# Projections with the weight as the stationary operand, log decays by a triangular matrix on TensorE, and a planner that chooses among 28 plans

## The chip, the cores and the metric

One core of a Trainium2 chip runs the whole step as one program. The metric is the device time in microseconds (us) of one execution; a run is quoted with the median of several.

## The reference, cut to what matters

Four layers, each a token mixer and then a SwiGLU feed-forward block, over two streams of 128 tokens of width 1024: context (s = 0) and latents (s = 1). All weights are float32.

```python
def swiglu(h, w_in, w_out):                      # D_FF = 2816, four layers
    gate, up = jnp.split(h @ w_in, 2, -1)
    return (jax.nn.silu(gate) * up) @ w_out

# layer 0, gated DeltaNet
q, k, v, z = jnp.split(h @ w_in, 4, -1)
qkv = jax.nn.silu(dwconv_centred(jnp.concatenate([q, k, v], -1), conv_w))   # 3 taps along the tokens

# layer 3, RWKV-7
r, k, v = jnp.einsum('sbtd,sde->sbte', xm[:3], w_rkv)
w = -jax.nn.softplus(-(w0[:, None, None, :] + lora(xm[3], w1, w2, jnp.tanh))) - 0.5
decay = jnp.exp(-jnp.exp(w.astype(F32)))         # per token, channel and direction
a = jax.nn.sigmoid(a0[:, None, None, :] + lora(xm[4], a1, a2, lambda x: x))
```

Layers 1 and 2 are a neighbourhood attention and a latent attention. Layers 0 and 3 are linear recurrences in both directions, computed per head as one block of 128 tokens: products between the tokens, the inverse of a unit triangular matrix, and products with it.

## The kernel before

**Two steps.** The model's code does not issue instructions. `Tape` records them, `Plan` (line 1652) orders them, `emit` (line 2009) issues them in that order, so every instruction has the line of `emit`, 2032 (2103 in the changed kernel). `Plan` is a list scheduler: each operation has a cost and a rank (the length of the work behind it), each engine takes the ready operation of highest rank, and tiles come from rooms with fixed numbers of slots (`ROOM`, line 501: 25 of `b`, 128x1024 float32, three of `ada`, 128x2048, seven PSUM banks `acc`). `best(rounds, waits)` (line 1970) plans forwards, takes new ranks from a walk backwards, and repeats; with `ROUNDS = 9` and one value of `WAIT`, 1800, it makes nine plans, and `trunk_kernel` emits the shortest by the planner's own count. Every engine then runs its list in order.

**Weights.** A weight tile comes in by a transfer on SyncE's queue, and `split` (line 261) makes two tiles of it in the fast float32r type: `hi`, a rounded copy by ScalarE (ACT), and `lo`, the rest, by VectorE (DVE). Each product is then three multiplies on TensorE (PE): x_hi with hi, x_hi with lo, x_lo with hi. Multiplies in plain float32, as in RWKV, run as two passes each; a transpose is one pass.

**`linear` (line 296), token-major.** For each 512 columns of the weight and each stream the activations, 128x128, are stationary and the weight's 512 columns move. The result has tokens on the partitions. Stream 1 follows stream 0 by a lag of some weight tiles (`FIN`, `IN`), which hold their slots until then.

**FFN, `ffn_` (line 453).** `w_in` is taken in 11 chunks of 512, gate and up in turn, the last chunk 256 of each. Gate goes through Silu on ACT, up is multiplied on DVE, and `to_T` (line 360) transposes the 128x512 result on PE (four transposes) and splits it for `linear_k` with `w_out`.

**DeltaNet, `deltanet_` (line 637).** `w_in` has eight chunks: q, k, v two each, then z. `evac` (line 733) copies a chunk, transposes it to channel-major, does the three taps there (one ACT and two DVE instructions for each of four blocks), applies Silu and transposes back. `unit` normalises and transposes q and k; the score products follow (PE, 128x256 plain float32), then the inverse (`inverses`, line 583): two STREAM_TRANSPOSEs on DVE, a serial chain of 62 small DVE instructions (`substitute`), two more transposes, then 256 PE passes of 32x32 (`inverse_64`).

**RWKV, `rwkv_` (line 1188).** Channel halves g = 0, 1 and directions d = 0, 1. `rw_decays` (line 1402) makes, channel-major, the log decay and a: for each of w and a, four 64-row multiplies and four Tanh; for w then a sum along the tokens by scans on DVE, the subtraction of the middle token's value, and exponentials. `rw_keys`, `rw_products` and `inverse` follow, once for g = 0 and once for g = 1; `core(g, d)` uses the results.

**Filler.** `ada_group` (line 217) makes the modulation vectors of this and the next layer: 32 multiplies for a group, four to each 1 MB tile of `ada_w`. `fill` records two or three groups in each mixer, and the planner sets them where it likes.

Of the kernel before, what the change touches and what calls it, by code (L numbers as in the profile page):

```python
# [18 lines left out]
FF = 2816  # L19
# [77 lines left out]
class Trunk:  # L97
# [224 lines left out]

    def linear_k(self, W, xs, evac, lags=None, done=None, whole=False):
# [129 lines left out]
    def ffn_(self, l):  # L453
# [5 lines left out]
        chunks = []  # L459
        for c in range(5):  # L460
            chunks += [[(c * 512, c * 512 + 512)], [(FF + c * 512, FF + c * 512 + 512)]]
        chunks += [[(2560, FF), (FF + 2560, 2 * FF)]]
        sil = {}

        def evac(ci, s, ps):
            if ci < 10 and ci % 2 == 0:
                sil[s] = self.g([128, 512])
                nc.scalar.activation(sil[s], ps, AF.Silu)
                return
            c = ci // 2  # L470
            if c == len(hid):
                hid.append([self.g([128, 4, 2, 128], F32R) for _ in range(2)])
            with self.scope():
                m = self.g([128, 512])
                if ci < 10:
                    nc.vector.tensor_tensor(m, ps, sil[s], op=OP.mult)
                    self.free(sil[s])
                    n = 4
                else:
                    t = self.g([128, 512])  # L480
                    nc.scalar.activation(t[:, :256], ps[:, :256], AF.Silu)
                    nc.vector.tensor_tensor(m[:, :256], ps[:, 256:], t[:, :256], op=OP.mult)
                    n = 2
                self.to_T(m, n, hid[c][0][:, :n, s, :], hid[c][1][:, :n, s, :])
        self.linear(W, chunks, xs, evac, FIN)
# [23 lines left out]
ROUNDS = 9  # L509
WAIT = 1800.0  # L510
# [5 lines left out]
class DeltaNet:  # L516
# [120 lines left out]
    def deltanet_(self, l):  # L637
# [95 lines left out]
        def evac(ci, s, ps):  # L733
            which, half = ci // 2, ci % 2
            if which == 3:
                nc.scalar.activation(zs[s][half].rearrange("p a b -> p (a b)"), ps, AF.Silu)
                return
            with self.scope():
                tok = self.g([128, 512])
                nc.scalar.activation(tok, ps, AF.Copy)  # L740
                p = self.ps()
                for i in range(4):
                    nc.tensor.transpose(p[:, i * 128:(i + 1) * 128], tok[:, i * 128:(i + 1) * 128], self.ident)
                x = p.rearrange("p (a b) -> p a b", b=128)
                cv = self.g([128, 4, 128])
                for i in range(4):
                    c = ci * 4 + i
                    nc.scalar.activation(cv[:, i], x[:, i], AF.Copy, scale=cw[:, 1, c:c + 1])
                    nc.vector.scalar_tensor_tensor(cv[:, i, 1:], x[:, i, :127], cw[:, 0, c:c + 1], cv[:, i, 1:], op0=OP.mult, op1=OP.add)
                    nc.vector.scalar_tensor_tensor(cv[:, i, :127], x[:, i, 1:], cw[:, 2, c:c + 1], cv[:, i, :127], op0=OP.mult, op1=OP.add)  # L750
                nc.scalar.activation(cv, cv, AF.Silu)
                p = self.ps()
                for i in range(4):
                    nc.tensor.transpose(p[:, i * 128:(i + 1) * 128], cv[:, i], self.ident)
                h0 = half * 4
                dst = (qk[s][which][:, h0:h0 + 4] if which < 2 else V[s][half]).rearrange("p a b -> p (a b)")
                nc.scalar.activation(dst, p, AF.Copy)
                if which < 2:
                    sq = self.g([128, 512])
                    nc.scalar.activation(sq, p, AF.Square)  # L760
                    nc.vector.tensor_reduce(ss[:, s, which, h0:h0 + 4], sq.rearrange("p (a b) -> p a b", b=128), axis=AX.X, op=OP.add)
            if ci == 3:
                unit(s)
            if ci == 5 and s == 1:
                decays()
# [33 lines left out]
        self.linear(I["dn_w_in"][j], [[(c * 512, c * 512 + 512)] for c in range(8)], xs, evac, IN)  # L799
# [380 lines left out]
class Rwkv:  # L1180
# [7 lines left out]
    def rwkv_(self, l):  # L1188
# [4 lines left out]
        r = self.g([96, 128])  # L1193
        for at, n, v in ((0, 48, I["rw_mu"][j].rearrange("i (k p) -> (i k) p", p=128)),
                         (48, 8, I["rw_k_a"][j].rearrange("(k p) -> k p", p=128)),
                         (56, 8, I["rw_r_k"][j].rearrange("(k e) d -> k (e d)", e=2)),
                         (64, 16, I["rw_w0"][j].rearrange("z (k p) -> (z k) p", p=128)),
                         (80, 16, I["rw_a0"][j].rearrange("z (k p) -> (z k) p", p=128))):
            nc.gpsimd.dma_start(r[at:at + n], v)
        p = self.ps()  # L1200
        nc.tensor.transpose(p[:, :96], r, self.ident[:96, :96])
        self.free(r)
        cols = self.g([128, 96])
        nc.vector.tensor_copy(cols, p[:, :96])
# [6 lines left out]
        self.rw_b0 = {"w": cols[:, 64:80].rearrange("p (z k) -> p z k", z=2), "a": cols[:, 80:96].rearrange("p (z k) -> p z k", z=2)}  # L1211
# [35 lines left out]
        wa = self.g([128, 2, 2, 128])  # L1247

        def lora(i, nm):
# [14 lines left out]
            t = hid[nm] = wa[:, "wa".index(nm)] if nm != "g" else self.g([128, 2, 128])  # L1264
# [78 lines left out]
        lora(4, "a")  # L1343
        k = project(1, mk, KLAGS)
# [25 lines left out]
        r = project(0, mr, RLAGS)  # L1370
# [6 lines left out]
        rT = features(r)  # L1377
# [24 lines left out]
    def rw_decays(self, g, d, hid, w2):  # L1402
# [5 lines left out]
        act = {}  # L1408
        for nm in "wa":
            o = self.g([128, 4, 2, 128])  # L1410
            for h in range(2):
                p = self.ps()
                for i in range(2):
                    nc.tensor.matmul(p[:, i * 256:i * 256 + 256], w2[nm][rows, (2 * h + i) * 128:(2 * h + i + 1) * 128],
                                     hid[nm][rows].rearrange("p s t -> p (s t)"), start=True, stop=True, tile_position=(64 * d, 0))
                for i in range(2):
                    c = g * 4 + 2 * h + i
                    nc.scalar.activation(o[:, 2 * h + i].rearrange("p s t -> p (s t)"), p[:, i * 256:i * 256 + 256], AF.Tanh,
                                         bias=self.rw_b0[nm][:, d, c:c + 1], scale=0.5)
            act[nm] = o  # L1420
        sg, al = act["w"], act["a"]
        seq = lambda t: t.rearrange("p c s t -> p (c s) t")

        cm = self.g([128, 4, 2, 128])
        fl = lambda t: t.rearrange("p c s t -> p (c s t)")
        nc.vector.tensor_scalar(fl(sg), fl(sg), 1.0, None, op0=OP.add)
        a, b = (fl(sg), fl(cm)) if d == 0 else (fl(sg)[:, ::-1], fl(cm)[:, ::-1])
        shp = [128, 8, 128]
        for h in (0, 512):
# [631 lines left out]
```

## Time and profile before

| | us |
|---|---|
| median of 3 runs | 1683.51 (1679.96 to 1689.08) |
| the profiled execution | 1688.48 |
| its span | 1686.7 |
| PE busy | 1587.1 (94%) |
| DVE busy | 1128.2 (67%) |
| ACT busy | 830.3 (49%) |

The times below are of the profiled execution, from the start of its span. A PE row's length runs from the start of its first multiply to the modelled end of the last, and multiplies overlap: a long run divided by its count gives their spacing, while the mean time of one is longer. Of the layers, the DeltaNet mixer takes about 0 to 277 us, RWKV about 1160 to 1490; FFN blocks lie at about 277, 630, 963 and 1491.

### The profile page before, as it was taken

How to read it: one execution, taken by the hardware profiler on the slowest of the kernel's cores; microseconds unless marked ns; L12 is line 12 of the kernel's file. 1: busy time of each engine (PE TensorE's matmuls, PEld its weight loads, DVE VectorE, ACT ScalarE, POOL GpSimd, SP SyncE). 2: the span in 40 equal slices, each digit the busy share in tenths (PEclk: the TensorE clock that was granted, in tenths of full speed). 3: DMA queues.
4: the chain of work that ended last, by engine and by line, in shares of the span. 5: the costliest groups of instructions: out<-in, count | busy, mean ns of one | idle time of the engine just before them, and what ended most of it. 6: DMA issues, size and time to landing. Idle time of an engine off the chain costs nothing.

```text
span 1686.7 us, 24968 instructions
## 1 busy us (share of the span) xinstructions
PE 1587.1 (94%) x9396; PEld 1206.5 (72%) x9396; DVE 1128.2 (67%) x2364; ACT 830.3 (49%) x1466; POOL 63.3 (4%) x109
## 2 busy tenths in 40 slices
PE   6999689999999899999998999999999499999998
PEld 2877267888767658887775688886657378878886
DVE  4788868545486675445798854548797878675554
ACT  4798166434455664444565644433545432354443
POOL 2001010000002000000000000001010010000000
PEclk9999899999999999999999999999998779999999
DMA  9665888545658684455767854557120452335553
GB/s 364 226 215 195 325 307 319 200 147 183 208 215 269 195 299 158 169 175 204 249 215 255 334 165 174 187 200 253 59 101 10 166 195 82 114 119 178 164 193 130
DMA packets 130601, 333.79 MB, mean 198 GB/s; under 512 B 18321, under 2 KB 32466, under 8 KB 119216
## 3 DMA queue, kind: packets, MB, share of 16 engines
q1 hardware_dynamic: 123888, 311.33, 52.4%
q0 software_dynamic: 6592, 20.86, 4.2%
q8 instruction: 74, 1.21, 0.3%
q14 instruction: 47, 0.39, 0.1%
HBM read 328.25 MB, written 3.90 MB: 197 GB/s over the span
## 4 chain that ended last, share of the span: by engine, by line
PE 73%; DVE 12%; DMA 8%; ACT 5%; issue 2%; SPq 0%; ACTq 0%; DVEq 0%
PE v L2032 73%; DVE v L2032 12%; DMA v<-ada_w 5%; ACT v L2032 4%; DMA v<-ffn_w_out 2%; DMA v<-na_w_qkv 1%; DMA v<-dn_w_in 1%; ACT L2032 0%; DMA v<-ffn_w_in 0%; SPq L2032 0%; ACTq L2057 0%; ACTq L2032 0%; DVEq L2032 0%
## 5 line engine op out<-in xcount | busy, mean ns | idle before, releaser
L2032 PE MATMUL v<-v,v 128*128 128x512 f32 (+13 forms) x9364 | 1582.6, 369 | 94.1 <-DVE v L2032 44.5
L2032 PEld LDWEIGHTS v<-v,v 128*128 128x128 f32 (+6 forms) x9364 | 1200.4, 170 | 473.2 <-issue 148.7
L2032 DVE TENSOR_TENSOR v<-v,v 128x512 f32<-128x512 f32 (+19 forms) x1271 | 864.4, 705 | 477.5 <-ACT v L2032 280.8
L2032 ACT ACTIVATE v<-v 128x512 f32<-128x512 f32 (+9 forms) x989 | 679.1, 721 | 797.2 <-PE v L2032 373.6
L2032 ACT ACTIVATE v<-v,v 128x128 f32<-128x128 f32 (+2 forms) x212 | 77.3, 413 | 30.4 <-PE v L2032 12.5
L2032 DVE SCALAR_TENSOR_TENSOR v<-v,v,v 128x127 f32<-128x127 f32 (+4 forms) x200 | 66.9, 381 | 7.1 <-ACT v L2032 6.1
L2032 ACT ACTIVATE v<-v,v,v 128x128 f32<-128x128 f32 (+2 forms) x136 | 55.4, 476 | 23.6 <-DVE v L2032 23.3
L2032 DVE TENSOR_REDUCE v<-v 128x4 f32<-128x512 f32 (+4 forms) x76 | 47.1, 626 | 18.0 <-PE v L2032 12.9
L2032 POOL DMA_DIRECT2D v<-v x22 | 11.8, 535 | 780.5 <-PE v L2032 633.9
L2032 DVE TENSOR_SCALAR v<-v 128x1 int32<-128x1 int32 (+9 forms) x194 | 32.8, 175 | 9.1 <-ACT v L2032 6.1
L2032 DVE SCALAR_TENSOR_TENSOR v<-v,v 128x1 f32<-128x1 f32 (+7 forms) x156 | 32.6, 218 | 4.8 <-ACT v L2032 2.2
L2032 ACT ACT_TABLE_LOAD x22 | 28.2, 1283 | 2.4 <-DVE v L2032 1.4
L2032 POOL MEMSET v<- 128x512 f32 (+3 forms) x26 | 15.6, 618 | 330.4 <-PE v L2032 182.4
L2032 DVE SCALAR_TENSOR_TENSOR v<-v 128x1 f32<-128x1 f32 (+4 forms) x171 | 26.2, 159 | 2.5
L2032 DVE TENSOR_SCALAR v<-v,v,v 128x128 f32<-128x128 f32 x64 | 25.0, 404 | 2.0 <-PE v L2032 1.5
L2032 DVE STREAM_TRANSPOSE v<-v 128x1024 f32<-128x1024 f32 x12 | 23.4, 2003 | 3.8 <-ACT v L2032 3.6
L2032 DVE TENSOR_SCALAR v<-v,v 128x512 f32<-128x512 f32 (+2 forms) x68 | 24.6, 395 | 0.4
L2032 DVE TENSOR_TENSOR v<-v 128x1 f32<-128x1 f32 (+4 forms) x74 | 11.7, 160 | 10.9 <-ACT v L2032 9.7
L2032 DVE COPY v<-v 128x32 f32<-128x32 f32 (+9 forms) x34 | 7.5, 223 | 12.8 <-PE v L2032 12.6
L2032 ACT ACTIVATION_READ_ACCUMULATOR v<-v,v 128x1 f32 x64 | 13.3, 208 | 0.0
L2032 DVE TENSOR_TENSOR_SCAN v<-v,v 128x512 f32<-128x512 f32 x8 | 9.2, 1206 | 0.1
L2032 PE MATMUL v<-v 128*128 128x256 f32 x32 | 8.0, 378 | 0.0
(39 smaller groups left out, 62.5 us busy)
## 6 DMA issues: line engine op xcount, KB each, us to landing
v<-ada_w SPq DMA_DIRECT2D x88, 1024.0 KB
v<-ffn_w_in SPq DMA_DIRECT2D x160, 512.0 KB
v<-ffn_w_out SPq DMA_DIRECT2D x88, 512.0 KB
v<-dn_w_in SPq DMA_DIRECT2D x32, 512.0 KB
v<-na_w_qkv SPq DMA_DIRECT2D x24, 512.0 KB
v<-rw_w_rkv SPq DMA_DIRECT2D x24, 512.0 KB
v<-v POOLq DMA_DIRECT2D x20, 512.0 KB, 7.0
v<-ada_w SPq DMA_DIRECT2D x16, 512.0 KB
```

What stands on the lines that cost most here:

```text
L2032: ins = getattr(getattr(nc, engine), method)(*[real(a) for a in args], **{k: real(a) for k, a in kw.items()}).ins
```

## The change

1. `linear_T` is new: the weight's 128x128 blocks are stationary, and the activations of both streams (256 columns) move. The result is channel-major, for both streams at once, and there is no lag.
2. FFN: the first pair of chunks (`TM = 1`) stays token-major; the other ten chunks go through `linear_T`, and their result needs no transpose.
3. DeltaNet: q, k and v go through `linear_T`; the first copy and transpose go, and the taps are taken for both streams in one instruction. z stays token-major.
4. RWKV: `w0` becomes a row of the weight (a row of ones in `hid`). The log decay is made token-major by one multiply for each stream, and the sum along the tokens, relative to the middle one, by four multiplies with a triangular matrix `rw_tri`. The scans, the subtraction and some copies go; POOL sets the middle column to 1. The r projection is done channel-major, and its transposes go.
5. The planner makes 14 rounds for each of two waits, 28 plans.

```diff
+    def linear_T(self, W, chunks, ht, evac):
+        ...
+        for ci, chunk in enumerate(chunks):
+            ...
+            banks = [self.ps() for _ in range(width // 256)]
+            for k0 in range(0, nk, 2):
+                hi, lo = self.weight([W[k0 * 128:(k0 + 2) * 128, a:b] for a, b in pieces], 2, width)
+                for kk in range(2):
+                    ...
+                        nc.tensor.matmul(o, hi[:, kk, c], xh, start=(k == 0 and i % 2 == 0), stop=False)
+                        nc.tensor.matmul(o, hi[:, kk, c], xl, start=False, stop=False)
+                        nc.tensor.matmul(o, lo[:, kk, c], xh, start=False, stop=(k == nk - 1 and i % 2 == 1))
+                self.free(hi, lo)
+            evac(ci, banks)
...
-        self.linear(W, chunks, xs, evac, FIN)
+        self.linear(W, [[x] for c in range(TM) for x in pair(c)], xs, evac, FIN)
...
+        self.linear_T(W, [x for c in range(TM, 5) for x in pair(c)] + [[(2560, FF), (FF + 2560, 2 * FF)]], ht, evac)
...
-ROUNDS = 9
-WAIT = 1800.0
+TM = 1
+ROUNDS = 14
+WAITS = (900.0, 3000.0)
...
-                tok = self.g([128, 512])
-                nc.scalar.activation(tok, ps, AF.Copy)
-                p = self.ps()
-                for i in range(4):
-                    nc.tensor.transpose(p[:, i * 128:(i + 1) * 128], tok[:, i * 128:(i + 1) * 128], self.ident)
...
-                    nc.vector.scalar_tensor_tensor(cv[:, i, 1:], x[:, i, :127], cw[:, 0, c:c + 1], cv[:, i, 1:], op0=OP.mult, op1=OP.add)
+                    nc.vector.scalar_tensor_tensor(cv[:, i, :, 1:], x[:, :, :127], cw[:, 0, c:c + 1], cv[:, i, :, 1:], op0=OP.mult, op1=OP.add)
...
+        self.linear_T(W, [(c * 512, c * 512 + 512) for c in range(6)], ht, evac)
+        self.linear(W, [[(c * 512, c * 512 + 512)] for c in (6, 7)], xs, gating, IN)
...
-        for h in (0, 512):
-            nc.vector.tensor_tensor_scan(b[:, h:h + 512], self.seg, a[:, h:h + 512], 0.0, op0=OP.mult, op1=OP.add)
...
+            nc.tensor.matmul(p, hid["w"][d][:, s], w2["w"][d], start=True, stop=True)
+            with self.scope():
+                sg = self.g([128, 512])
+                nc.scalar.activation(sg, p, AF.Tanh, scale=0.5)
+                nc.vector.tensor_scalar(sg, sg, 1.0, None, op0=OP.add)
+                q = self.ps()
+                for c in range(4):
+                    nc.tensor.matmul(q[:, c * 128:c * 128 + 128], sg[:, c * 128:c * 128 + 128], self.rw_tri[:, d], start=True, stop=True)
+            q = q.rearrange("p (c t) -> p c t", c=4)
+            nc.scalar.activation(AR[s][:, :, 1], q, AF.Exp, scale=-KAPPA / 2)
+            nc.scalar.activation(cm[:, :, s], q, AF.Exp, scale=KAPPA / 2)
...
+            nc.gpsimd.memset(AR[s][:, :, 1, m:m + 1], 1.0)
+            nc.gpsimd.memset(cm[:, :, s, m:m + 1], 1.0)
...
-        r = project(0, mr, RLAGS)
+        rT = project_T(0, mr)
...
-    _, order, turns, _ = min(Plan(tape).best(ROUNDS, (WAIT,)), key=lambda x: x[0])
+    _, order, turns, _ = min(Plan(tape).best(ROUNDS, WAITS), key=lambda x: x[0])
```

The new plan moves work on every engine. Three places on PE, where `out<-moving or weight tiles` carry running numbers. In the first FFN block, the kernel before has stretches of 128x512, and two transposes (`v_75` is the identity matrix) between two chunks:

```order
L2032 MATMUL v_3382<-v_3311,v_2729 128x512
L2032 MATMUL v_3382<-v_3296,v_2815 128x512
L2032 MATMUL v_3382<-v_3296,v_2729 128x512
L2032 MATMUL v_3382<-v_3311,v_2729 128x512
L2032 MATMUL v_3382<-v_3296,v_2815 128x512
L2032 MATMUL v_3417<-v_75,v_3054 128x128 x2
L2032 MATMUL v_3422<-v_3238,v_2721 128x512
L2032 MATMUL v_3422<-v_3244,v_2721 128x512
L2032 MATMUL v_3422<-v_3238,v_2796 128x512
```

The changed kernel has the same products as 128x256, and no transpose behind the first pair of chunks:

```order
L2103 MATMUL v_3379<-v_2826,v_3307 128x256
L2103 MATMUL v_3379<-v_2875,v_3307 128x256
L2103 MATMUL v_3379<-v_2826,v_3320 128x256
L2103 MATMUL v_3366<-v_2826,v_3307 128x256
L2103 MATMUL v_3366<-v_2875,v_3307 128x256
L2103 MATMUL v_3366<-v_2826,v_3320 128x256
L2103 MATMUL v_3366<-v_2826,v_3307 128x256
L2103 MATMUL v_3366<-v_2875,v_3307 128x256
L2103 MATMUL v_3366<-v_2826,v_3320 128x256
```

In DeltaNet, just ahead of the first 32x32 of the inverse. 32x512 are the filler, 128x128 products with the initial state, `v_75` transposes. Before:

```order
L2032 MATMUL v_1671<-v_1779,v_63 32x512 x4
L2032 MATMUL v_1822<-v_1791,v_63 32x512 x4
L2032 MATMUL v_1822<-v_1804,v_63 32x512 x4
L2032 MATMUL v_1845<-v_1537,v_1212 128x128
L2032 MATMUL v_1845<-v_1562,v_1212 128x128
L2032 MATMUL v_1845<-v_1537,v_1212 128x128
L2032 MATMUL v_1845<-v_1562,v_1212 128x128
L2032 MATMUL v_1822<-v_1813,v_63 32x512 x4
L2032 MATMUL v_1822<-v_1847,v_63 32x512 x4
L2032 MATMUL v_1888<-v_75,v_1819 128x128 x4
L2032 MATMUL v_1822<-v_1861,v_63 32x512 x4
L2032 MATMUL v_1905<-v_1855,v_1479 32x32 x4
```

Changed:

```order
L2103 MATMUL v_1863<-v_1629,v_1364 128x128
L2103 MATMUL v_1870<-v_1614,v_1364 128x128
L2103 MATMUL v_1870<-v_1629,v_1364 128x128
L2103 MATMUL v_1870<-v_1614,v_1364 128x128
L2103 MATMUL v_1870<-v_1629,v_1364 128x128
L2103 MATMUL v_1900<-v_1780,v_63 32x512 x4
L2103 MATMUL v_1900<-v_1798,v_63 32x512 x4
L2103 MATMUL v_1900<-v_1815,v_63 32x512 x4
L2103 MATMUL v_1941<-v_75,v_1897 128x128 x4
L2103 MATMUL v_1900<-v_1919,v_63 32x512 x4
L2103 MATMUL v_1900<-v_1933,v_63 32x512 x4
L2103 MATMUL v_1988<-v_1957,v_1568 32x32 x6
```

Between the last score product (128x256) and the first 32x32 stood 64 filler multiplies, 20 of z (128x512), 32 with the state and four transposes; now 48 filler, 48 of z, 24 with the state and eight transposes: 28 z multiplies moved behind the scores, 16 filler multiplies moved behind the inverse.

In RWKV, ahead of the first 32x32 of the second inverse (g = 1). 128x64 and 64x64 belong to `core(0, 1)`. Before:

```order
L2032 MATMUL v_12097<-v_11065,v_11018 128x256
L2032 MATMUL v_12101<-v_11065,v_11018 128x256
L2032 MATMUL v_12097<-v_11065,v_11018 128x256
L2032 MATMUL v_12101<-v_11065,v_11018 128x256
L2032 MATMUL v_12109<-v_11065,v_11018 128x256 x2
L2032 MATMUL v_10675<-v_12056,v_63 32x512 x4
L2032 MATMUL v_10675<-v_12068,v_63 32x512 x4
L2032 MATMUL v_12195<-v_12190,v_11931 32x32 x8
L2032 MATMUL v_12195<-v_12190,v_11940 32x32 x8
```

Changed:

```order
L2103 MATMUL v_13477<-v_13516,v_12383 64x64
L2103 MATMUL v_13493<-v_12674,v_13462 128x64 x4
L2103 MATMUL v_13455<-v_13486,v_63 32x512 x4
L2103 MATMUL v_13477<-v_13542,v_12479 64x64 x8
L2103 MATMUL v_13570<-v_75,v_13452 128x128 x4
L2103 MATMUL v_13578<-v_12286,v_12241 128x256
L2103 MATMUL v_13581<-v_12286,v_12241 128x256
L2103 MATMUL v_13578<-v_12286,v_12241 128x256
L2103 MATMUL v_13581<-v_12286,v_12241 128x256
L2103 MATMUL v_13493<-v_13516,v_13490 128x64 x8
L2103 MATMUL v_13455<-v_13533,v_63 32x512 x4
L2103 MATMUL v_13607<-v_13585,v_13246 32x32 x8
```

Between the last product that feeds the inverse and its first 32x32 stood 20 filler multiplies and 45 others (122 passes in all); now 56 filler multiplies and 112 others (328 passes): most of `core(0, 1)` and 36 more filler multiplies moved here.

## Rows read from the trace of the kernel before

**Rows 1.** The page: span and PE's busy time.
```profile
span 1686.7 us, 24968 instructions
...
PE 1587.1 (94%) x9396; PEld 1206.5 (72%) x9396; DVE 1128.2 (67%) x2364; ACT 830.3 (49%) x1466; POOL 63.3 (4%) x109
```

**Rows 2.** Who PE waited for, whole run: total us, times, longest.
```profile
PE v L2032 <- DVE v L2032: 44.5, 24, 21.9
PE v L2032 <- DMA v<-ada_w: 19.4, 18, 3.3
```

**Rows 3.** Stretches: length, busy us of PE, PEld, DVE, ACT, POOL; clock, DMA share, GB/s.
```profile
277.00:427.00 150.00, 150.00 (x673) 122.58 (x674) 82.48 (x86) 65.14 (x82) 1.07 (x2) 1.00 0.55 189
...
1320.00:1357.00 37.00, 13.22 (x236) 10.63 (x236) 33.45 (x72) 11.02 (x22) 0.54 (x1) 0.64 0.42 162
```

**Rows 4.** Timeline of PE, float32r runs and transposes: start, us, what, count.
```profile
299.73 30.44 PE L2032 MATMUL v<-v,v 128*128 128x512 f32 x132
...
838.16 4.40 PE L2032 MATMUL v<-v,v 128*128 128x288 f32 x32
...
43.77 0.64 PE L2032 MATMUL v<-v,v 128*128 128x256 f32 x4
...
401.05 1.36 PE L2032 MATMUL v<-v,v 128*128 128x128 f32 x11
```

**Rows 5.** PE by form, 43.70 to 44.20 us: busy us, mean ns of one.
```profile
L2032 PE MATMUL v<-v,v 128*128 128x256 f32 x6 | 0.9, 287 | 0.0
```

**Rows 6.** Timeline of PE, runs of plain float32 passes (two to a multiply).
```profile
1216.12 15.18 PE L2032 MATMUL v<-v,v 128*128 128x512 f32 x35
...
1188.26 4.91 PE L2032 MATMUL v<-v,v 128*128 128x256 f32 x22
...
1193.75 1.78 PE L2032 MATMUL v<-v,v 64*128 64x256 f32 x14
...
1316.73 2.35 PE L2032 MATMUL v<-v,v 128*32 128x512 f32 x20
```

**Rows 7.** DVE by form, whole run: busy us, mean ns, idle before.
```profile
L2032 DVE TENSOR_TENSOR v<-v,v 128x512 f32<-128x512 f32 x326 | 214.2, 685 | 126.0 <-PE v L2032 107.8 <-ACT v L2032 10.2 <-DMA v<-na_rel_bias 5.7
...
L2032 DVE SCALAR_TENSOR_TENSOR v<-v,v,v 128x127 f32<-128x127 f32 x96 | 29.2, 344 | 6.5 <-ACT v L2032 5.7
...
L2032 DVE TENSOR_TENSOR_SCAN v<-v,v 128x512 f32<-128x512 f32 x8 | 9.2, 1206 | 0.1
...
L2032 DVE SCALAR_TENSOR_TENSOR v<-v,v,v 128x256 f32<-128x256 f32 x42 | 17.5, 478 | 0.1
```

**Rows 8.** Timeline of PE around DeltaNet's inverse; the brackets give the wait before.
```profile
156.66 0.81 PE L2032 MATMUL v<-v 128*128 128x256 f32 x3
...
203.52 1.51 PE L2032 MATMUL v<-v,v 128*32 128x512 f32 x8 [3.31 <-DMA v<-ada_w]
```

**Rows 9.** Who PE waited for from 164 to 205 us.
```profile
PE v L2032 <- DMA v<-ada_w: 9.3, 5, 3.3
PE v L2032 <- DVE v L2032: 5.7, 2, 4.9
```

**Rows 10.** Timeline of DVE: the last transposes of DeltaNet's inverse.
```profile
193.66 3.90 DVE L2032 STREAM_TRANSPOSE v<-v 128x1024 f32<-128x1024 f32 x2
```

**Rows 11.** Timeline of PE around RWKV's second inverse.
```profile
1321.89 8.40 PE L2032 MATMUL v<-v,v 128*128 128x64 f32 x76 [2.37 <-ACT v L2032]
1352.18 1.03 PE L2032 MATMUL v<-v,v 32*32 32x32 f32 x31 [21.89 <-DVE v L2032]
```

**Rows 12.** Timeline of DVE in the same stretch: the inverse itself.
```profile
1321.25 3.92 DVE L2032 STREAM_TRANSPOSE v<-v 128x1024 f32<-128x1024 f32 x2 [2.93 <-ACT v L2032]
...
1326.64 23.35 DVE L2032 TENSOR_TENSOR v<-v,v 128x31 f32<-128x31 f32 x62
1350.02 3.79 DVE L2032 STREAM_TRANSPOSE v<-v 128x1024 f32<-128x1024 f32 x2
```

**Rows 13.** Timeline of POOL in RWKV: a transfer, the wait ahead of it.
```profile
1313.35 0.55 POOL L2032 DMA_DIRECT2D v<-rw_ln_b  x1 [18.23 <-DVE v L2032]
```

More of the change, by code (lines that the diff above doesn't have):

```diff
@@ L458, in ffn_ @@
         hid = []
[L459 to L462, printed above, removed]
+        pair = lambda c: [(c * 512, c * 512 + 512), (FF + c * 512, FF + c * 512 + 512)]
         sil = {}
         def evac(ci, s, ps):
-            if ci < 10 and ci % 2 == 0:
+            if ci % 2 == 0:
                 sil[s] = self.g([128, 512])
@@ L755, in evac @@
[L755 to L761, printed above, removed]
+                for s in range(2):
+                    p = self.ps()
+                    for i in range(4):
+                        nc.tensor.transpose(p[:, i * 128:(i + 1) * 128], cv[:, i, s], self.ident)
+                    dst = (qk[s][which][:, h0:h0 + 4] if which < 2 else V[s][half]).rearrange("p a b -> p (a b)")
+                    nc.scalar.activation(dst, p, AF.Copy)
+                    if which < 2:
+                        sq = self.g([128, 512])
+                        nc.scalar.activation(sq, p, AF.Square)
+                        nc.vector.tensor_reduce(ss[:, s, which, h0:h0 + 4], sq.rearrange("p (a b) -> p a b", b=128), axis=AX.X, op=OP.add)
+                        self.free(sq)
@@ L762, in evac @@
             if ci == 3:
-                unit(s)
-            if ci == 5 and s == 1:
+                unit(0)
+                unit(1)
+            if ci == 5:
                 decays()
@@ L1246, in rwkv_ @@
         hid = {}
-        wa = self.g([128, 2, 2, 128])
+        hid["w"] = [self.g([128, 2, 128]) for _ in range(2)]
+        for d in range(2):
+            nc.gpsimd.memset(hid["w"][d], 0.0)
+            nc.gpsimd.memset(hid["w"][d][64 - 64 * d:65 - 64 * d], 1.0)
         def lora(i, nm):
@@ L1263, in lora @@
             self.free(w)
-            t = hid[nm] = wa[:, "wa".index(nm)] if nm != "g" else self.g([128, 2, 128])
+            if nm == "w":
+                for d in range(2):
+                    rows = slice(64 * d, 64 * d + 64)
+                    nc.scalar.activation(hid["w"][d][rows].rearrange("p s t -> p (s t)"), acc[rows, :256], AF.Tanh)
+                return
+            t = hid[nm] = self.g([128, 2, 128])
             f = t.rearrange("p s t -> p (s t)")
@@ L1407, in rw_decays @@
         rows = slice(64 * d, 64 * d + 64)
[L1408 to L1420, printed above, removed]
```

150 lines of the change are left out of this document (96 added, 54 removed).

## The prediction

> **What bounds the kernel now.** I read the page first [rows 1]: TensorE (PE) is busy for 1587.1 of 1686.7 us. The list of waits [rows 2] tells what holds PE in the rest: DVE for 44.5 us, of which one wait alone is 21.9, and transfers of `ada_w`, the filler's weights, for 19.4. The stretches [rows 3] show the two kinds of place. In an FFN block PE is busy for 150.00 of 150.00 us: there only PE's own instructions count, and work taken from DVE or ACT is worth nothing. From 1320 to 1357 us PE is busy for 13.22 of 37.00: there the serial inverse on DVE counts, and what the planner puts under it. So the change has two questions: does PE's own work become less, and does the new order cover the two inverses better?
>
> **PE's own work, step by step.** Transposes: 36 go in each FFN block, 48 in DeltaNet, 16 in RWKV, 208 in all. A run of eleven took 1.36 us [rows 4]. Multiplies overlap, so a run of n ends one multiply's own length, about 0.29 us [rows 5], after the last of n - 1 spacings: the transposes stand (1.36 - 0.29)/10 = 0.11 us apart. PE is busy around them, so the whole counts: 208 x 0.11 = 22.9 us less.
>
> Narrow multiplies: 2016 float32r multiplies of 512 columns (432 in each FFN block, 288 in DeltaNet) become 4032 of 256. The 512s stand (30.44 - 0.29)/131 = 0.2302 us apart. For 256 columns the trace has four in a row at full clock: (0.64 - 0.29)/3 = 0.118, on three intervals only. The 288s have more: (4.40 - 0.29)/31 = 0.1326. The line through 288 and 512 has 0.436 ns a column and meets 256 at 0.119 [rows 4, 5]. I take 0.118: two cost 0.236 for one of 0.2302, and 2016 x 0.0058 = 12 us more. The ends: half of a 512, 0.1151, would make this 0; the 288s' own spacing would make it 2016 x (0.2652 - 0.2302) = 71 us more.
>
> What could hurt is the weight load, since each multiply has its own and there are twice as many. The rows say that it hides: the same line leaves 7 ns a multiply at no columns, and a transpose, 128 columns with a load of its own, already stands 0.11 from the next [rows 4]. So the load's floor is at most 0.11, under 0.118, but only just.
>
> The Trainium skill ("TensorE: Matmul & The Clock Gate", section "The mechanism") speaks against this change: a weight load overlaps running multiplies only where the row group differs, which full-height blocks never give. The trace disagrees, with those 7 ns.
>
> RWKV's decays: in each of the four cases of g and d two plain 512s and eight plain 128s come in, 16 and 64 passes in all. At 15.18/35 = 0.43 and at 0.11 (taken from the transposes, also one pass of 128) that is 6.9 + 7.0 = 13.9 us. Sixteen half-height multiplies, 32 passes, go; those run two abreast, 1.78/14 = 0.13 each, 4.1 us. So +9.8 us. The r projection turns 64 passes of 512 into 128 of 256: 64 x 0.43 = 27.5 against 128 x 0.216 = 27.6, nothing [rows 6].
>
> The sum of PE's work: -22.9 + 12 + 9.8 = -1. By place it is -5.8 in the four FFN blocks together (144 x 0.11 less 1728 x 0.0058), -3.6 in DeltaNet and +8.0 in RWKV.
>
> **DVE and ACT.** The taps on 256 columns instead of 128 save 96 x 0.344 - 48 x 0.478 = 10 us of DVE, the scans 8 x 1.206 = 9.6 [rows 7]. I cost this at nothing by itself: PE covers it. It counts only where it starts an inverse earlier, which is in the next two terms. If PE's cover were gone in DeltaNet or RWKV, these 20 us are the most that it would be worth.
>
> **DeltaNet's inverse.** The last score product ends at 156.66 + 0.81 = 157.5; the filler group that stands last before the 32x32 ends at 203.52 + 1.51 = 205.0 [rows 8]. DVE had the inverse ready at 193.66 + 3.90 = 197.6 [rows 10], so PE was 7.5 us late, and it was so because its list stood still on `ada_w` for 9.3 us and on DVE for 5.7 [rows 9]. The new order has 12 tiles of filler there instead of 16 and 28 more z multiplies, whose weights come on the same queue but ahead. PE's work in the stretch stays near 28 us. At best the stretch shrinks by the 7.5 us, since DVE's 40 us from the scores to the inverse stay; at worst the four tiles put off cost the same waits later, four at the mean of 9.3/5 = 1.9 us, which is +7.4 with nothing gained. I take -5.
>
> **RWKV's second inverse.** From the first transpose at 1321.25 to the first 32x32 at 1352.18 is 30.9 us of DVE, and the serial chain of 62 takes 23.35 of them [rows 12]. PE had 8.40 us of work, waited 2.37 before it and 21.89 after it: 24.3 us lost [rows 11]. The new order puts 328 passes under this inverse where 122 stood. The run of 76 mixed passes took 8.40 us and the filler 2.35 us for 20 passes, some 0.11 us each [rows 6, 11], so the added 206 are worth about 20 us. Against that, eight 128x512 DVE instructions of `core` now stand inside the serial chain: at 0.685 us [rows 7], 5.5 us. So of 24.3 us lost about 10 remain, and I take -13. The ends: -20 (all 20 us fit, and the eight fit into gaps) and -3 (the added work waits for its own chain of PE, ACT and DVE, as `core` does elsewhere). What is late next is that chain, or the 14 filler tiles of this stretch. Three lie ready in their slots; at 162 GB/s for a share of 0.42 [rows 3] the queues would give some 386 GB/s at a full share (an estimate), and 11 tiles of 1.05 MB then take 30 us, less than the stretch has.
>
> The clock was 0.64 of full speed from 1320 to 1357 [rows 3], after PE had stood still; with the hole mostly filled some of that work runs at 2.4 instead of 1.2 GHz. Of 13.22 busy us I take 2 back (0 to 4).
>
> **The sum.** -1 - 5 - 13 - 2 = -21 us. The profiled execution took 1688.48 us and its span 1686.7, so 1.8 us lie around it, which the change does not touch: 1667.5 for that execution. The median of the runs is 5.0 us below it: 1662.5, say 1663. The order of everything else is new too. Of the waits in [rows 2], 17 us on DVE and 10 on `ada_w` lie outside the two inverses; I let the new plan win or lose a third, 8 us either way.
>
> **Rivals.** First, slower: the narrow multiply is bound by its weight load. At 0.118 the load's 0.11 hides by 8 ns, and any unevenness between the two shows at once. The price is 4032 times what it stands above 0.118: at the 288s' 0.1326 [rows 4] +59 us, 1722. From 0.123 on the 21 us are gone, from 0.126 it is slower than before by over 0.5%. For it: over four in ten of PE's multiplies would sit so near the floor, and the only direct reading has three intervals. Against: the 288s, with a load each, show none of it. 6%.
>
> Second, the same: the holes are filled with work that waits itself, so that the gain at both inverses is 3 us, and PE's own work gives 1: about 1680. For it: work under an inverse needs DVE, which the inverse holds. Against: the moved work in RWKV is mostly multiplies and filler. 13%.
>
> Third, POOL: it now sets the middle column of each decay, and `rw_keys` on DVE waits for that. In the new order the last four of g = 1 stand behind a transfer of `rw_ln_b`, before which POOL waited for 18.23 us [rows 13]. Were that wait to fall there, keys and the second inverse would be late by up to 18 us: 1681. The transfer waits for a slot, and nothing says that it comes late again: 4%.
>
> Fourth, slower by far: each load runs by itself ahead of its multiply. With the transposes' 0.11 for a load, 2016 more loads are +222 us, 1885. The 288s and 512s, 7 ns a multiply beyond their columns [rows 4], speak against it: 1%. (It is what the rule of the Trainium skill above would give.)
>
> Fifth, better: the second inverse is covered wholly (-20), DeltaNet's wait goes (-7.5), and the plan wins its 8 elsewhere: about 1643. 12%.
>
> **How the numbers follow.** The forecast, 1663 with its own range of 1650 to 1675, has 62%; the same-cases 17%, the better case 12%, the two cases of the load 7%, and 2% that the plan is worse elsewhere by more than 28 us. A measurement of this kernel tells a change of about 0.5% (8.4 us: 1675 and 1692) from none. Faster is the forecast and the better case, 74%; same 17%; slower 9%. The range leaves out the load and part of the better case: 1641 to 1684.
>
> **What would show it.** The 256-column runs of the profile after: 0.118 us apart, with PE full in the FFN blocks and each some 1 us shorter. Between the last product and the first 32x32 of the second RWKV inverse, a wait on DVE near 10 us instead of 24.3. In DeltaNet the first 32x32 no later than 8 us behind DVE's last transpose. The prediction is wrong if the 256s stand at 0.123 or more, if PE's waits under the second inverse stay above 20 us, or if waits for `ada_w` grow by more than they lose.

## The result, and the profile after

The changed kernel takes 1661.05 us in the median of four runs (1651.9 to 1672.64), 0.9881 of the kernel before, 95% interval 0.9833 to 0.9928: 1.2% faster, which is clear of the noise, and 2 us from the forecast of 1663. The profiled execution took 1662.25 us.

The page of the changed kernel answers to [rows 1]. PE stands idle for 79.5 us (1660.5 - 1581.0) instead of 99.6, so 20 of the 26.2 us of span are idle time of PE:

```profile
span 1660.5 us, 28763 instructions
...
PE 1581.0 (95%) x11316; PEld 1295.0 (78%) x11316; DVE 1098.4 (66%) x2276; ACT 813.7 (49%) x1407; POOL 70.8 (4%) x136
```

Who PE waited for in the whole run (total us, times, longest) answers to [rows 2]: DVE 30.9 instead of 44.5, and no wait of 21.9 any more; `ada_w` 17.0 instead of 19.4, ACT 14.6 instead of 18.3.

```profile
PE v L2103 <- DVE v L2103: 30.9, 26, 8.6
PE v L2103 <- DMA v<-ada_w: 17.0, 17, 4.5
PE v L2103 <- ACT v L2103: 14.6, 15, 3.2
```

PE by form from 282 to 304 us, within the first FFN block, where only the new form runs (count, busy us, mean ns of one): (22.4 - 0.281)/187 = 0.1183 us apart, as forecast [rows 4].

```profile
L2103 PE MATMUL v<-v,v 128*128 128x256 f32 x188 | 22.4, 281 | 0.0
```

Two stretches of the changed kernel, a part of the first FFN block and the time from the first transpose to the first 32x32 of RWKV's second inverse (length, busy us of PE, PEld, DVE, ACT, POOL; clock, DMA share, GB/s), answer to [rows 3]. PE is still full in the FFN block. In the second, 30.18 of 36.90 us are busy, where it was 13.22 of 37.00 in [rows 3], and the clock is 0.81 instead of 0.64. The stretch from the first transpose to the first 32x32 itself became 6.0 us longer (36.9 instead of 30.9).

```profile
266.70:416.00 149.30, 148.96 (x1080) 138.43 (x1081) 78.49 (x77) 65.16 (x78) 1.11 (x2) 1.00 0.63 206
1306.20:1343.10 36.90, 30.18 (x258) 16.80 (x259) 34.27 (x76) 6.01 (x11) 1.06 (x2) 0.81 0.86 323
```

The timelines of the same place, PE and then DVE (start, us, what, count, the wait before), answer to [rows 11] and [rows 12]: the listed waits are five short ones, 7.0 us together, where it was 24.3. But DVE now does other work within the serial chain (the row of 58 and the next, 64x512, of `core`), and reaches its last transposes 27.89 us after the chain's start (1311.47 to 1339.36) instead of 23.38: 4.5 us more, where the prediction had 5.5.

```profile
1307.97 7.75 PE L2103 MATMUL v<-v,v 64*128 64x128 f32 x78 [2.00 <-ACT v L2103]
1317.12 1.07 PE L2103 MATMUL v<-v,v 128*32 128x512 f32 x8 [1.40 <-DMA v<-ada_w]
1319.61 1.94 PE L2103 MATMUL v<-v,v 128*32 128x512 f32 x8 [1.42 <-DMA v<-ada_w]
1322.88 1.11 PE L2103 MATMUL v<-v,v 64*64 64x64 f32 x8 [1.34 <-DVE v L2103]
1324.78 23.40 PE L2103 MATMUL v<-v,v 128*32 128x512 f32 x321 [0.79 <-DVE v L2103]
```

```profile
1306.24 3.77 DVE L2103 STREAM_TRANSPOSE v<-v 128x1024 f32<-128x1024 f32 x2 [3.96 <-ACT v L2103]
...
1311.47 23.54 DVE L2103 TENSOR_TENSOR v<-v,v 128x31 f32<-128x31 f32 x58
1335.60 3.73 DVE L2103 TENSOR_TENSOR v<-v,v 64x512 f32<-64x512 f32 x12 [0.59 <-PE v L2103]
1339.36 3.72 DVE L2103 STREAM_TRANSPOSE v<-v 128x1024 f32<-128x1024 f32 x2
```

DeltaNet's inverse in the changed kernel, PE and then DVE, answers to [rows 8] and [rows 10]; the last row is DVE's first transposes in the kernel before. The 152 begin with 16 passes of filler; the first 32x32 starts at 195.1, 2.2 us behind DVE's last transpose (189.19 + 3.69 = 192.9), where it was 7.4. Yet from the end of the last score product, 145.8, it is 49.3 us, where it was 47.5, and PE's waits in it are 15.7 us (the three in brackets below and one of 1.33 on ACT) instead of 15.0 [rows 9]: the hole did not shrink. What PE gained at the end DVE lost at the front: it reached its first transpose 14.0 us after the scores (159.76), against 6.5 before, and its row of 155.91 stands behind a wait of 4.22 us on PE. So DVE's way from the scores to the inverse, 40 us that the prediction took to stay, became 47.1.

```profile
144.78 1.03 PE L2103 MATMUL v<-v 128*128 128x256 f32 x4
...
180.56 5.18 PE L2103 MATMUL v<-v,v 128*32 128x512 f32 x24 [8.57 <-DVE v L2103]
187.11 1.65 PE L2103 MATMUL v<-v,v 128*128 128x128 f32 x12 [1.36 <-DVE v L2103]
193.24 6.94 PE L2103 MATMUL v<-v,v 128*32 128x512 f32 x152 [4.48 <-DMA v<-ada_w]
```

```profile
155.91 2.41 DVE L2103 TENSOR_TENSOR v<-v,v 128x256 f32<-128x256 f32 x7 [4.22 <-PE v L2103]
...
159.76 3.88 DVE L2103 STREAM_TRANSPOSE v<-v 128x1024 f32<-128x1024 f32 x2
...
189.19 3.69 DVE L2103 STREAM_TRANSPOSE v<-v 128x1024 f32<-128x1024 f32 x2
```

```profile
163.97 3.94 DVE L2032 STREAM_TRANSPOSE v<-v 128x1024 f32<-128x1024 f32 x2 [0.38 <-ACT v L2032]
```

**Where the 26.2 us of span went.** The stages are cut at the first multiply of each FFN block; filler is what the plan moved from one stage to another, at 0.11 us a pass; edits is the prediction's sum of PE's work; the rest is the difference.

| stage | before, us | after, us | change | filler | edits | rest |
|---|---|---|---|---|---|---|
| start and DeltaNet | 277.0 | 266.7 | -10.3 | -7.0 | -3.6 | +0.3 |
| first FFN, neighbourhood attention | 353.0 | 341.3 | -11.7 | +3.5 | -1.5 | -13.7 |
| second FFN, latent attention | 333.5 | 330.5 | -3.0 | -0.9 | -1.5 | -0.6 |
| third FFN, RWKV | 528.0 | 530.1 | +2.1 | +4.4 | +6.6 | -8.9 |
| last FFN | 195.2 | 191.9 | -3.3 | 0 | -1.5 | -1.8 |

The largest gain stands at the neighbourhood attention, in which the change edits nothing. Who PE waited for there, before (427 to 630 us) and after (416 to 608 us): 14.1 us became 7.3, which is half of the stage's rest of 13.7. The granted clock went from 0.96 to 1.00 over some 200 us.

```profile
PE v L2032 <- ACT v L2032: 9.5, 6, 6.3
PE v L2032 <- DMA v<-ada_w: 2.7, 2, 2.3
PE v L2032 <- DVE v L2032: 1.9, 5, 0.9
```

```profile
PE v L2103 <- ACT v L2103: 3.1, 3, 1.8
PE v L2103 <- DVE v L2103: 2.3, 2, 1.7
PE v L2103 <- DMA v<-ada_w: 1.9, 2, 1.4
```

The clock can account for the other half. These are three stretches of that stage at the lower level (0.50) in the kernel before, one of the next stage, and then the neighbourhood attention after (length, PE busy, clock, DMA share, GB/s). PE was busy for 13.8 us of the three. A filler pass stands 0.11 us from the next in [rows 6]; from 890.3 to 893.3 us, at 0.50, sixteen passes fill the 3.00 us, some 0.2 us each. At half the speed, 13.8 us hold 6.9 us of work, so about 7 us came back (an estimate).

```profile
473.70:480.50 6.80, 6.35 (x21) 0.50 1.00 402
552.20:559.00 6.80, 4.37 (x9) 0.50 0.18 67
620.40:623.80 3.40, 3.05 (x11) 0.50 1.03 414
890.30:893.30 3.00, 3.00 (x16) 0.50 0.25 36
```

```profile
416.00:608.00 192.00, 183.02 (x1026) 1.00 0.77 256
```

### The profile page after: what moved, and what is told of

Same layout as the page of the kernel before. It is cut to its first block, busy times and chain, and to the rows that moved or that the text cites. A ratio compares the mean times of both kernels' runs of the same rounds, so it can differ in the third digit from the quotient of the medians.

```text
span 1660.5 us, 28763 instructions
## 1 busy us (share of the span) xinstructions
PE 1581.0 (95%) x11316; PEld 1295.0 (78%) x11316; DVE 1098.4 (66%) x2276; ACT 813.7 (49%) x1407; POOL 70.8 (4%) x136
## 4 chain that ended last, share of the span: by engine, by line
PE 75%; DMA 11%; DVE 9%; ACT 4%; issue 1%; SPq 0%; POOL 0%; ACTq 0%; DVEq 0%
PE v L2103 75%; DVE v L2103 9%; DMA v<-ada_w 4%; DMA v<-ffn_w_out 4%; ACT v L2103 4%; DMA v<-dn_w_in 1%; DMA v<-na_w_qkv 1%; DMA v<-na_rel_bias 0%; DMA new_state_dn<-v 0%; DMA v<-mla_w_q_b 0%; ACT L2103 0%; DMA v<-ffn_w_in 0%; SPq L2103 0%; POOL v L2103 0%; ACTq L2128 0%
## 5 line engine op out<-in xcount | busy, mean ns | idle before, releaser
L2103 PE MATMUL v<-v,v 128*128 128x256 f32 (+16 forms) x11284 | 1576.5, 332 | 73.9 <-DVE v L2103 30.9
L2103 PEld LDWEIGHTS v<-v,v 128*128 128x128 f32 (+7 forms) x11284 | 1289.1, 172 | 358.6 <-issue 98.3
L2103 DVE TENSOR_TENSOR v<-v,v 128x1024 fp32r<-128x1024 f32 (+16 forms) x1243 | 856.7, 714 | 486.9 <-ACT v L2103 319.3
L2103 ACT ACTIVATE v<-v 128x1024 fp32r<-128x1024 f32 (+14 forms) x972 | 674.9, 733 | 788.1 <-PE v L2103 258.0
L2103 ACT ACTIVATE v<-v,v 128x128 f32<-128x128 f32 (+2 forms) x172 | 65.4, 440 | 31.0 <-DVE v L2103 22.5
L2103 DVE SCALAR_TENSOR_TENSOR v<-v,v,v 128x128 f32<-128x128 f32 (+4 forms) x152 | 58.9, 438 | 9.8 <-ACT v L2103 7.6
L2103 POOL MEMSET v<- 128x512 f32 (+5 forms) x48 | 20.3, 434 | 418.1 <-PE v L2103 215.8
L2103 DVE SCALAR_TENSOR_TENSOR v<-v,v 128x8 f32<-128x8 f32 (+6 forms) x156 | 32.3, 217 | 4.1 <-ACT v L2103 2.2
L2103 ACT ACTIVATION_READ_ACCUMULATOR v<-v,v 128x1 f32 x64 | 13.7, 214 | 0.0
L2103 DVE COPY v<-v 128x32 f32<-128x32 f32 (+7 forms) x22 | 4.4, 206 | 8.5 <-PE v L2103 8.4
L2103 POOL DMA_DIRECT2D v<-rw_w x10 | 6.0, 600 | 63.4 <-DVE v L2103 62.3
```

The lines of the kernel that those rows point to most:

```text
L2103: ins = getattr(getattr(nc, engine), method)(*[real(a) for a in args], **{k: real(a) for k, a in kw.items()}).ins
```

## The experiments

The table of stages set the question: are the gaps smaller because of the edits, or because the search drew a better plan? Theory A is the prediction's: the edits let the holes be covered. Theory B: the search did it. Every kernel below is planned anew. One table holds all results. The count is the planner's own length of the plan that it chose. The ratio is to the kernel before, which ran beside each kernel on the same chip; the runs come from several chips, so ratios compare better than times. Work and gaps are read from each trace: the interval from one multiply's start to the next counts as work up to the usual spacing of its form (0.231 us for 512 columns, 0.174 for 384, 0.133 for 288, 0.118 for 256, 0.11 for the others; plain float32 0.429 for 512 and 0.216 for 256), and what is over is gap; some 14 us lie before and behind. Time lost to the lower clock counts as gap, and so does nearly half of the filler's own time (four passes that run abreast take some 0.43 us, of which 0.25 count as work) in every kernel alike, so only differences between rows mean something. Work and gaps are those of one execution: the changed kernel's four executions, of the same plan, went from 1651.9 us at a mean clock of 0.984 to 1672.64 at 0.974.

| kernel | plans | count | ratio, 95% interval | work, us | gaps, us |
|---|---|---|---|---|---|
| before | 9 | 1628.0 | 1 | 1450.3 | 222.7 |
| plan28 | 28 | 1618.9 | 0.9951 (0.9918 to 0.9985) | 1450.8 | 207.7 |
| before_6000 | 200 | 1603.8 | 0.9892 (0.9839 to 0.9946) | 1455.8 | 200.8 |
| nine | 9 | 1628.5 | 1.0017 (0.9988 to 1.0046) | 1445.5 | 228.7 |
| changed | 28 | 1602.2 | 0.9881 (0.9833 to 0.9928) | 1447.8 | 198.9 |
| after_4000 | 200 | 1598.8 | 0.9803 (0.9778 to 0.9828) | 1448.9 | 190.1 |
| no_ffn | 28 | 1627.3 | 0.9930 (0.9897 to 0.9963) | 1454.0 | 208.6 |
| no_ffn_1800 | 200 | 1613.1 | 0.9962 (0.9934 to 0.9990) | 1452.3 | 201.6 |
| no_rwkv | 28 | 1610.8 | 0.9973 (0.9936 to 1.0011) | 1439.0 | 228.6 |
| no_rwkv_6000 | 200 | 1595.2 | 0.9826 (0.9787 to 0.9866) | 1443.0 | 199.0 |
| no_rwkv_tm2 | more | 1588.2 | 0.9751 (0.9720 to 0.9781) | 1437.2 | 185.6 |
| no_delta_1500 | 200 | 1607.9 | 0.9889 (0.9853 to 0.9924) | 1450.6 | 199.8 |
| only_ffn_6000 | 200 | 1601.1 | 0.9958 (0.9920 to 0.9996) | 1451.4 | 210.9 |

Those with 200 plans carry the shortest of 20 rounds for each of ten waits; the number in the name is the wait at which it was found. For `no_rwkv_tm2` the search went wider, over other waits and over `TM` as well.

**The search alone (`plan28`), and the edits alone (`nine`).** To the kernel before (the call takes `WAITS` in place of `(WAIT,)`), and to the changed one:

```diff
-ROUNDS = 9
-WAIT = 1800.0
+ROUNDS = 14
+WAITS = (900.0, 3000.0)
```

```diff
-ROUNDS = 14
-WAITS = (900.0, 3000.0)
+ROUNDS = 9
+WAITS = (1800.0,)
```

> The kernel before with its planner alone changed: the shortest of 28 plans instead of 9, no instruction of the model changed. By the planner's own count the plan is 9 us shorter (1618.9 instead of 1628.0). Theory A (the edits to the model shape the work so that the holes under the inverses can be covered; the search adds 8 us either way): 1674 to 1690, and under RWKV's second inverse TensorE still stands still for 20 us or more. Rival B (the search is what gained): 1657 to 1668. If it is between, 1668 to 1674, both have a share.

> The changed kernel with the planner as before: nine plans, a wait of 1800. By the planner's own count its best plan is 26 us longer than that of the changed kernel (1628.5 instead of 1602.2) and no shorter than that of the kernel before (1628.0). Theory A: the model's edits carry most of the gain, so 1661 to 1672, with little of the wait under RWKV's second inverse back. Rival B (the search gained it): 1676 to 1690, the gain is gone.

The search alone gives half a per cent (1678.42 us, within theory A), the edits alone nothing (1688.5 us, as rival B has it). Neither theory stands: the two add up to 0.3%, together they measured 1.2%. `nine` has every instruction of the changed kernel and 30 us more of gaps. Under its second inverse (1325.1 to 1369.5 us) PE waits for 19.1 us:

```profile
PE v L2103 <- DVE v L2103: 11.0, 1, 11.0
PE v L2103 <- DMA v<-ada_w: 5.2, 2, 3.4
PE v L2103 <- ACT v L2103: 2.9, 1, 2.9
```

**One edit taken back at a time (`no_ffn`, `no_rwkv`).** To the changed kernel; the rest of `ffn_`, or of the RWKV functions, as in the kernel before:

```diff
-        self.linear(W, [[x] for c in range(TM) for x in pair(c)], xs, evac, FIN)
...
-        self.linear_T(W, [x for c in range(TM, 5) for x in pair(c)] + [[(2560, FF), (FF + 2560, 2 * FF)]], ht, evac)
+        self.linear(W, chunks, xs, evac, FIN)
```

```diff
-        rT = project_T(0, mr)
+        r = project(0, mr, RLAGS)
...
+            nc.vector.tensor_tensor_scan(b[:, h:h + 512], self.seg, a[:, h:h + 512], 0.0, op0=OP.mult, op1=OP.add)
```

> The changed kernel with the feed-forward blocks as before (all of w_in token-major, with the transposes), planned anew over 28 plans; DeltaNet and RWKV stay changed. Theory A: only TensorE's own work comes back, 5.8 us in four blocks, so 1661 + 6 = 1667, and each block 1 to 2 us longer. Rival C (the feed-forward edit gives more than its own work, since linear_T holds no weight tiles for a lag and leaves DVE and ACT free for what comes next): 1673 or more, and the time comes back outside the blocks, in the mixers that follow them.

> The changed kernel with the RWKV layer as before (scans on VectorE, the r projection token-major), planned anew over 28 plans; the feed-forward blocks and DeltaNet stay changed. Theory A as predicted: TensorE's work falls by 8.0 us, and the wait under the second inverse is back, 13 us and 2 of clock, so 1661 - 8 + 15 = 1668. Rival D (the 28 plans cover the inverse as well without the edit, which then only costs its 8 us of TensorE's work): 1653, with the wait on DVE under the second inverse near 10 us.

`no_ffn` took 1676.63 us, which is rival C's number (that the time came back in the mixers, as C has it, is not shown), `no_rwkv` 1681.45, which is slower than either expected. PE's work moved as forecast, +6.2 and -8.8 us against +5.8 and -8.0; the rest is gaps, +10 and +30. In `no_rwkv` the wait under the second inverse (1308.7 to 1340.5 us) is back, as theory A has it, but that is about half of the 30:

```profile
PE v L2069 <- DVE v L2069: 18.5, 1, 18.5
```

So taking one edit back tells its work and little else, because the plan is drawn again.

**The same search for every kernel.** `before_6000`, `after_4000` and `no_rwkv_6000` differ from the above in two numbers only, `ROUNDS` 20, 16 and 12 and one wait of 6000, 4000 and 6000:

> The kernel before, no instruction of the model changed, with the best of 20 plans for a wait of 6000: by the planner's count 1603.8, nearly that of the changed kernel (1602.2). If the planner's count decides what the chip takes, whatever the model's instructions (theory B, the search): 1659 to 1667. If the edits are needed for the holes (theory A): 1673 or more, with over 20 us of TensorE standing still under RWKV's second inverse, as in both plans of that model seen so far (22.6 and 21.2).

> The changed kernel with the best of 16 plans for a wait of 4000: by the planner's count 1598.8, 3.4 us under the changed kernel's plan. Theory B (the count decides): 1655 to 1662. Rival E (a plan's count tells its time on the chip to no better than 10 us, and the changed kernel's 1661 was a lucky draw among them): anywhere from 1662 to 1685, with TensorE's own work the same to 2 us and only its gaps different.

> The changed kernel with RWKV as before, with the best of 12 plans for a wait of 6000: by the planner's count 1595.2, the shortest of all looked at, and 8.8 us less work on TensorE than the changed kernel by the trace of the first such kernel. Theory B: 1650 to 1656, and it would beat both kernels. Rival E: 1665 to 1685. If the hole under RWKV's second inverse is again over 20 us while the changed kernel has 11.7, the RWKV edit is what lets it be filled.

The kernel before reaches 1668.83 us with no edit at all, just past theory B's range but nearer to it than to theory A, and it fills the second inverse nearly wholly. Its ratio, 0.9892, can't be told from that of the changed kernel, 0.9881. PE's waits on DVE in that kernel, whole run, and from 1300 to 1339.2 us:

```profile
PE v L2032 <- DVE v L2032: 27.2, 24, 4.5
...
PE v L2032 <- DVE v L2032: 1.7, 2, 1.1
```

So the hole of [rows 11] was a matter of the plan, not of RWKV's instructions, and theory A falls there. The changed kernel's better plan took 1654.2, just under theory B's range; `no_rwkv_6000` took 1657.62, between the two expectations and nearer to theory B's, with 13.5 us of waits under its second inverse.

**What each edit is worth under that search.** `no_delta_1500` and `no_ffn_1800` take one edit back from the changed kernel, `only_ffn_6000` gives the kernel before the FFN edit alone, `no_rwkv_tm2` is `no_rwkv` with:

```diff
-TM = 1
-ROUNDS = 14
-WAITS = (900.0, 3000.0)
+TM = 2
+ROUNDS = 15
+WAITS = (5000.0,)
```

> The changed kernel with DeltaNet as before (feed-forward blocks and RWKV changed), with the shortest of 200 plans by the planner's count (20 rounds for each of ten waits; it is found at a wait of 1500): 1607.9, against 1598.8 for the best of 200 of the changed kernel, which took 1654.2. In the nine kernels so far the chip took 60 us more than the count, give or take 6. Theory G (with a wide search each edit is worth what the count says): 1668, 14 us above the changed kernel's best. Rival (only TensorE's own work of that edit comes back, 3.6 us): 1658. TensorE's work should be 3 to 5 us above the changed kernel's either way.

> The changed kernel with the feed-forward blocks as before (DeltaNet and RWKV changed), with the shortest of 200 plans by count (at a wait of 1800): 1613.1. Theory G: 1673, 19 us above the best plan of the changed kernel. Rival (only TensorE's own work, 5.8 us, comes back): 1660.

> The kernel before with the feed-forward edit alone, with the shortest of 200 plans by count (at a wait of 6000): 1601.1, against 1603.8 for the kernel before with the same search, which took 1668.8. Theory G: 1661. Rival (TensorE's own work alone, 5.8 us): 1663, which is the same here; what would speak against both is a time of 1669 or more: then the feed-forward edit by itself gives nothing and pays only beside the DeltaNet edit.

> RWKV as before, DeltaNet changed, feed-forward blocks changed with two pairs of chunks token-major instead of one, and the plan with the shortest count of all looked at, 1588.2 (at a wait of 5000). Theory G: 1648 (1642 to 1654), faster than every kernel so far; TensorE's work about 8 us below the changed kernel's. Rival E (a count under 1600 is luck of the count and not of the chip): 1655 or more.

`no_ffn_1800` (1672.71 us) fits theory G. `no_delta_1500` is undecided: its median, 1659.37, fits the rival (work alone), but its ratio, 0.9889, is 14 us behind the 0.9803 of the changed kernel's best plan, with intervals that do not meet, and that is theory G's distance. `only_ffn_6000` (1678.1) fits neither: alone, the FFN edit is 0.7% behind the kernel before under the same search, but the two intervals overlap, so a loss is not shown. The RWKV edit gives nothing that can be told from noise under that search: 0.9826 without it, 0.9803 with it, and the intervals overlap. `no_rwkv_tm2` took 1638.92 us, under its range, and beats both kernels: its interval, 0.9720 to 0.9781, lies wholly under the changed kernel's. It differs from the changed kernel in three things, RWKV as before, `TM`, and a wider search, and no run separates them. Its page:

```profile
span 1636.6 us, 27826 instructions
...
PE 1567.3 (96%) x10868; PEld 1265.1 (77%) x10868; DVE 1106.3 (68%) x2296; ACT 816.2 (50%) x1402; POOL 63.4 (4%) x109
```

Over all thirteen kernels the time follows the count, 0.85 us for each 1 (a straight line through the table, with the ratio times 1683 us), but scatters by 7 us around it. Two kernels with a plan each can therefore differ by some 10 us (7 x 1.4) that the count does not tell, whatever the reason. The 15 us between the kernel before and the changed one under the same search (0.9892 and 0.9803) are more than that, and these two kernels do differ, but not by enough to settle what the edits are worth beyond their work. The FFN edit shows it: beside the others it gains 0.5% (with overlapping intervals) and 1.6%, alone nothing.

**The price of a narrow multiply (`widths`).** This kernel leaves out the whole model, and only runs multiplies behind one another:

```diff
+    for n, count, lhs, rhs in [(512, 120, W, x)] + [(n, 96, W, x) for n in WIDTHS] + ...:
+        for c in range(count):
+            nc.tensor.matmul(acc[c % 2][:, :n], lhs[:, c % 8], rhs[:, :n], start=(c < 2), stop=(c >= count - 2))
```

> A kernel that computes nothing of the model: one 128x1024 weight in the fast float32 type, and behind one another on TensorE 120 multiplies of 512 columns, then 96 each of 384, 320, 288, 272, 256, 240, 224, 192, 160, 128 and 64 columns, each with a weight load of its own (eight blocks in turn, two PSUM banks in turn), then 48 plain float32 multiplies each of 256, 128 and 64 columns; the outputs are zeros. It measures the price that the prediction took from three intervals. Theory A: spacing is 7 ns and 0.436 ns a column down to a floor set by the weight load at 0.11 or below, so 0.230, 0.174, 0.147, 0.133, 0.126, 0.118 at 256, and from 240 down the floor, somewhere from 0.06 to 0.11. First rival: the floor lies just under 256 and is felt above it, 0.123 or more at 256. Fourth rival: each load adds its own time, 0.2 or more at 256.

PE by form, each row from a window of its own (count, busy us, mean ns of one):

```profile
L2032 PE MATMUL v<-v,v 128*128 128x320 f32 x77 | 11.5, 309 | 0.0
L2032 PE MATMUL v<-v,v 128*128 128x256 f32 x78 | 9.5, 283 | 0.0
L2032 PE MATMUL v<-v,v 128*128 128x240 f32 x83 | 9.5, 275 | 0.0
L2032 PE MATMUL v<-v,v 128*128 128x128 f32 x83 | 9.4, 275 | 0.0
```

The spacings are (11.5 - 0.309)/76 = 0.147, 0.120, 0.1125 and 0.111 us. From 320 to 256 columns the slope is 0.42 ns a column; 128 columns cost nearly what 240 do. There is a floor at 0.111, and the 256s stand 0.009 above it. The first and the fourth rival are out, and the 8 ns of margin that the prediction had read off three intervals are right.

That floor fits the Trainium skill ("TensorE: Matmul & The Clock Gate", section "LDWEIGHTS (loading the stationary operand)"), which gives a load of 128 columns 128/1.2 ns, an estimate of 0.107 us. The same page's section "Step-by-step: what each phase is for" lets a load into the background buffer overlap a running multiply; with 0.120 for a load and a multiply of 256 columns the trace agrees with that, and not with the rule that the prediction cited.

## Why the prediction was right, step by step

- **PE's own work: right to a few us.** -1 was forecast. The three plans of the kernel before average 1452.3 us of work, those of the changed kernel 1447.4: -5, where equal instructions spread by 3 us to either side. Taking the FFN edit back gave +5.8 (mean of two; forecast 5.8), DeltaNet +3.2 (3.6), RWKV -6.4 (mean of two; -8.0). Only the FFN edit alone (`only_ffn_6000`) falls short, 0.9 under that average instead of 5.8. The 256s stand at 0.118.
- **DVE and ACT at nothing: nothing speaks against it.** DVE's busy time fell by 29.8 us, and `nine`, with 24.3 us less of it than before, gained nothing.
- **DeltaNet's inverse, -5: wrong, 0.** The sign was read from how late PE was behind DVE; that lateness went, from 7.4 to 2.2 us, as the prediction wanted to see, but DVE itself came later after the scores, and its 40 us there did not stay (47.1). The criterion looked at one end of the stretch.
- **RWKV's second inverse, -13: near in size, wrong in cause.** PE's waits in the stretch fell from 24.3 to 7.0 us, but the stretch became 6.0 longer, and the rest of its stage in the table is -8.9. And the same instructions with nine plans left 19.1 us of waits, while the kernel before without any edit left 1.7 on DVE in its better plan.
- **The clock, -2: too small, and in the wrong place.** The mean granted clock went from 0.969 to 0.980. PE was busy at the lower level for 72 us before and 52 after, by the trace; at half speed that is some 10 of the 26 us (an estimate). About 7 of them lie in the neighbourhood attention; from the third FFN block to RWKV's end PE was busy at the lower level for 32 us before and 34 after, so nothing came back where the prediction had its 2.
- **"The new plan elsewhere", 8 us either way: the term that was mis-sized.** It gave 14 us at the first FFN block and the neighbourhood attention, about half by shorter waits and half by the clock (an estimate), and made up for DeltaNet. The search, point 5 of the change, has no term of its own in the sum. Of the changed kernel's three plans, `nine` at 1688.5, the measured one, and `after_4000` at 1654.2, one lies outside the range given. The sum came out by luck: the plan that was drawn happened to gain elsewhere what was missing here.
- **The rivals.** First and fourth: out by `widths`. Third: the last four of POOL's settings of the middle column (1283.38 to 1292.32) do stand behind a transfer of `rw_ln_b`, but POOL waited for 0.43 us before that one; the long wait, 9.35, came before the next, behind them (POOL's timeline: start, us, what, count, the wait before). So it cost nothing.

```profile
1279.27 0.68 POOL L2103 DMA_DIRECT2D v<-rw_ln_b  x1 [0.43 <-PE v L2103]
...
1292.32 0.11 POOL L2103 MEMSET v<- 128x4 f32 x1 [0.38 <-ACT v L2103]
1301.78 0.63 POOL L2103 DMA_DIRECT2D v<-rw_ln_b  x1 [9.35 <-DVE v L2103]
```

- The second (holes that refill) is what `nine` shows, though under another plan; the fifth (1643) is near what `no_rwkv_tm2` reached, without the RWKV edit and with another `TM` and search. The 74% for faster left little room for this: with the old number of plans the same edits were no gain.

What stays open: how much the edits give beyond their work at the best plan that each kernel could have, whether the FFN edit pays only beside the others or was unlucky alone, and which of its three differences makes `no_rwkv_tm2` the fastest.

## What to carry to other kernels

Where a search orders the instructions, the plan drawn is a term of its own, here about 7 us in one standard deviation around what the planner's count tells, and 34 us between two plans of the same instructions: compare kernels under the same search, with more than one plan each, before an edit is given the credit. Split the trace into work and gaps; here work could be forecast to some 5 us from spacings, gaps could not. When a plan shortens a wait at one end of a stretch, look at the whole stretch, from the last product that feeds it.

## What the runs showed of the hardware

Two things stand out. The floor under narrow multiplies, 0.111 us from 240 columns down, is so near that a moving side narrower than 256 columns would have cost nearly the same per multiply. And with float32r multiplies of 64 columns the granted clock fell although PE was never idle: in `widths`, 157 to 171 us (length, PE busy, clock, DMA share, GB/s), it is 0.64, a mean between its levels of 1.2 and 2.4 GHz, and behind them, with plain float32 multiplies of 256 columns, it is back at 0.99.

```profile
157.00:171.00 14.00, 14.00 (x85) 0.64 0.00 1
174.00:193.00 19.00, 19.00 (x89) 0.99 0.00 1
```
